# A diffusion backbone on one core: the first stage in one written order, with bands by row and scale and gates turned from columns

## The chip, the core and the metric

The kernel runs on one core of one Trainium2 chip. The time is device microseconds of one execution; the median of the runs is compared. The engines are named as the profile names them: PE (TensorE, matmuls), DVE (VectorE), ACT (ScalarE), POOL (GpSimd) and SP (SyncE, which issues the loads and stores here). SBUF is the memory that the engines work from, PSUM the banks that PE writes.

## The reference

512 latent tokens `x` and 256 context tokens `ctx`, each of 1024 features, go through two layers; everything is float32. Layer 0 mixes tokens by pooling, layer 1 by attention, and each is followed by an MLP of width 4096. Six vectors per layer (shift, scale and gate of the mixer and of the MLP) come from the conditioning, once for the latent and once for the context tokens. The first layer's mixer and what surrounds it:

```
sh1, sc1, gt1, sh2, sc2, gt2 = split(silu(c) @ w_ada[i] + b_ada[i], 6)      # c_ctx gives the context's
h   = rms_norm(x, g_mix_pre) * (1 + sc1) + sh1
# pooling: feature group g (256 features) averages over a window of 2, 4, 8 or 16 tokens
y   = concat_g((mean_g(h) - h)[:, group g] @ w_pool[g]) * pool_scale
x   = x + gt1 * rms_norm(y, g_mix_post)
m   = rms_norm(x, g_mlp_pre) * (1 + sc2) + sh2
x   = x + gt2 * rms_norm(square(relu(m @ w_in)) @ w_out, g_mlp_post)
```

`rms_norm(x, g)` is `x * rsqrt(mean(x*x) + eps) * g`. `pool_scale` and the gate `gt1` are vectors over the 1024 features, the same for all tokens of a kind.

## The kernel before, in words

Tokens stand in rows of 128: four latent rows (0 to 3) and two context rows (4 and 5), each a tile of 128 tokens by 1024 features in `xr`. Features are cut into eight tiles of 128 (k = 0 to 7), two for each window of the pooling. Matrix products whose weights are float32 are made of parts: weights and activations are split into a high part and a remainder (`hi`, `lo`), and three products of parts are added in PSUM.

The first stage is everything from the first load to the first group of the MLP's input matmuls. It runs thus:

- **Row norms.** Each row is loaded (`xload`, issued by SP), ACT squares and sums it, DVE adds epsilon, POOL raises to the power -0.5, and DVE writes the scaled row into `acc`. `rows_a` issues the first three, `rows_b` the last.
- **Bands.** The mean of a window minus the token itself is a product with a band matrix of 128 by 144. `band_mm(t, ks)` multiplies row t's feature tiles ks by it, into PSUM tiles named psm (latent) and psc (context), with features on the partitions; neighbouring rows add into the same columns, so a feature tile is complete when its last row is done. The bands of a first and of a last row have other edges: `band_edge(0)` and `band_edge(1)` each make a copy of the band and change its edge, both on DVE. `band_ev` moves the sums to SBUF.
- **Conditioning.** For each of the vectors PE multiplies weights from `w_ada` (1 MB per load, PSUM tile psada) by the conditioning; DVE adds rows, PE selects (`sel`), DVE and ACT finish.
- **Mixer.** The sums are scaled by 1 + sc1 and split (`hi` on ACT, `lo` on DVE), and multiplied by the split pooling weights (pspool). Before the split, the pooling weights are multiplied by `pool_scale`, which has to stand in every partition: `pool_weights` makes that by a matmul of a column of ones, on one partition, with the 4 KB row `scale_row` (psg).
- **Gates.** A gate is a column of 128 features per tile, and it is needed as a row in every partition. `gate_half(ci, h)` makes four tiles of it by a matmul of the column, read with a stride of 0 over 128 columns, with the identity (psg). The attention's gate (`gate_rows`, line 333) uses the same function.
- **Turns.** The rows are transposed for the MLP (psx), split, and its first group is multiplied (psin).

PE executes its instructions in one order, and the first stage's order is written out by hand. `Steps` holds pairs of a time and a function, and runs them sorted by that time; the string `FIRST` is a list of some 300 steps, each put in at 14.5 and a running thousandth. Ahead of these stand, by times of their own, the row norms, the bands of the first four feature tiles for the four latent rows, and the pool scale. While the stage is issued, PE, DVE and ACT are wrapped in `Kept`, which pins what they issue into program order (hence the many instructions whose line is that of this helper: 89 before, 91 after). Behind the stage a scheduler orders DVE and ACT.

Loads of weights go into two pools of buffers (`rawe` with four, `rawp` with three); which load of the first stage takes which is set by the list `turns`. PSUM is two double banks (psA) and four single ones (psB).

Of the kernel before, what the change touches and what calls it, by code (L numbers as in the profile page):

```python
# [9 lines left out]
F32 = mybir.dt.float32  # L10
# [3 lines left out]
ALU = mybir.AluOpType  # L14
# [27 lines left out]
ev:0* ev:2 psc0:4 psm:4 rb:5 wsc:0 psm:6 wsc:1 ev:4* wph:0 mm:SC1_0 wph:1 wpl:0 mm:SH1_0 ev:6* rows:SC1_0 wpl:1  # L42
psc0:5 sel:SC1_0 rows:SH1_0 evc:2* mods:SC1_0 evc:0* sel:SH1_0 mm:SC1_1 mods:SH1_0 hi:0 psc:4 rows:SC1_1 hi:1
psc:6 lo:0 mm:SH1_1 evc:4* lo:1 evc:6* sel:SC1_1 rows:SH1_1 pool:4:0 mods:SC1_1 sel:SH1_1 mm:SC1_2 mods:SH1_1
hi:2 pool:0:0 rows:SC1_2 pool:5:0 hi:3 lo:2 mm:SH1_2 lo:3 sel:SC1_2 rows:SH1_2 pool:4:1 mods:SC1_2 sel:SH1_2
ms:4:0 mm:SC1_3 mods:SH1_2 hi:4 c:4:0 pool:5:1 rows:SC1_3 mm:SH1_3 hi:5 lo:4 sel:SC1_3 pool:0:1 rows:SH1_3
mods:SC1_3 sel:SH1_3 lo:5 pool:1:0 pool:1:1 mods:SH1_3 pool:5:2 hi:6 mm:GT1_0a ms:1:0 lo:6 pool:4:2 hi:7
mm:GT1_0b c:1:0 lo:7 pool:0:2 mm:GT1_2a rows:GT1_0 pool:4:3 sel:GT1_0 ms:4:1 mm:GT1_2b w_in mods:GT1_0 gc:0:0
gc:1:0 c:4:1* rs:4 pool:0:3 rows:GT1_2 psg:0:0 ms:0 sel:GT1_2 psg:1:0 c:0* mods:GT1_2 rs:0 gc:0:1 gc:1:1 psg:1:1
gate:1:0 gate:0:0 pool:5:3 b:4:0 gate:1:1 b:1:0 mm:SC2_0a ms:5 b:4:1 psg:0:1 r:4 c:5* rs:5 pool:1:2 gate:0:1 b:5  # L50
mm:SC2_0b s:4 pool:1:3 r:5 whi:0 rs2:4 pool:3:0 ms:1:1 rows:SC2_0 pool:3:1 c:1:1* b:0 mm:SH2_0a rs:1 n:4*
sel:SC2_0 b:1:1 mm:SH2_0b s:5 r:0 pool:2:0 whi:1 rs2:5 pool:2:1 rows:SH2_0 pool:2:2 s:0 mods:SC2_0 r:1 sel:SH2_0
mm:SC2_2 n:5* rs2:0 mods:SH2_0 wlo:0 pool:2:3 s:1 turn:4:0 n:0 turn:4:1 ms:2 rs2:1 mm:SH2_2 h:4:1 h:4:0* rs:2
pool:3:2 n:1 xhi:4:0 mm:SC2_3 rows:SH2_2 xhi:4:1 rows:SC2_2 xlo:4:0 sel:SH2_2 turn:0:1 xlo:4:1 sel:SC2_2 h:0:1*
pool:3:3 mods:SH2_2 mods:SC2_2 turn:0:0 b:2 xhi:0:1 mm:SH2_3 ms:3 xlo:0:1 in:4:0:1 h:0:0* rows:SH2_3 rs:3
in:4:1:1 b:3 xhi:0:0 in:0:1:1 r:3 turn:0:2 in:4:0:0 h:0:2* xlo:0:0 in:4:1:0 s:3 r:2 in:0:1:0 in:0:0:1 xhi:0:2
rs2:3 wlo:1 s:2 in:0:0:0 turn:0:3 xlo:0:2 n:3* sel:SH2_3 rs2:2 turn:4:2 rows:SC2_3 in:0:2:0 mods:SH2_3 h:4:2*
n:2 sel:SC2_3 in:0:2:1 xhi:4:2 mods:SC2_3 turn:2:2 h:0:3 turn:4:3 h:2:2* turn:2:3 xlo:4:2 turn:2:1 xhi:2:2 h:4:3
in:4:2:1 h:2:1* in:4:2:0 xlo:2:2 xhi:4:3 h:2:3 turn:2:0 in:2:2:1 xhi:2:1 xlo:4:3 xhi:0:3 in:2:2:0 xlo:2:1 h:2:0*
in:4:3:1 xlo:0:3 in:2:1:0 xhi:2:0 xhi:2:3 in:0:3:1 xlo:2:0 xlo:2:3 in:0:3:0 in:4:3:0 in:2:0:0 in:2:3:0 in:2:0:1  # L60
in:2:3:1 in:2:1:1
# [31 lines left out]
def backbone(ctx: ExitStack, tc, x, ctx_in, w_ada, w_pool, pool_scale, w_qkv, g_q, g_k, w_o, w_mlp_in,  # L93
# [134 lines left out]
    given = phase[:, 16:32]  # L228
    sy.dma_start(given, vecs[:, 160:176])
# [10 lines left out]
    one = sm_tile("sm")  # L240
    ve.memset(one, 1.0)
# [87 lines left out]
    def gate_half(ci, h):  # L329
        ps = psB.tile([P, 512], F32, tag="b", name="psg")  # L330
        gc = halfgate.pop((ci, h))
        for k in range(4):
            te.matmul(ps[:, k * P:(k + 1) * P], gc[:, 4 * h + k:4 * h + k + 1].broadcast_to([P, P]), ident,
                      start=True, stop=True)
        halfgate[ci, h] = ps
# [105 lines left out]
    def band_edge(v):  # L441
        c = (HALO, P)[v]
        ve.tensor_copy(bands[:, v], bands[:, 2])
        ve.tensor_copy(bands[:, v, :, c:c + HALO], edges[:, v])

    band_edge(0)

    means, lat, con = {}, {}, {}

    def band_open(k):  # L450
        lat[k] = psA.tile([P, 2, 512], F32, tag="a", name="psm")
        for u in range(2):
            means[k + u] = lat[k][:, u, :], None

    def band_open_c(k):
        con[k] = psB.tile([P, 2, 256], F32, tag="b", name="psc")
        for u in range(2):
            means[k + u] = means[k + u][0], con[k][:, u, :]

    def band_mm(t, ks):  # L460
# [4 lines left out]
        for k in ks:  # L465
# [3 lines left out]
    def band_ev(k, q, on_act):  # L469
        to = accv[:, (0, NL)[q]:(NL, NT)[q], P * k:P * k + 256]  # L470
        (sc.copy if on_act else ve.tensor_copy)(to, (lat, con)[q][k].rearrange("p u (a n) -> p (u a) n", n=256))
        for u in range(2):
            means[k + u] = (means[k + u][0], to[:, u, :]) if q else (to[:, 2 * u:2 * u + 2, :], means[k + u][1])
# [1138 lines left out]
```

## Time and profile before

| what | us |
|---|---|
| median of 3 runs | 1158.05 (1158.02 to 1160.07) |
| the profiled execution | 1160.61 |
| its span | 1158.80 |
| PE busy (of the span) | 1142.9 (99%) |
| DVE busy | 932.9 (81%) |
| ACT busy | 632.8 (55%) |
| end of the first stage: the second group of the MLP's input matmuls starts on PE | 96.58 |

The page's first part gives each engine's busy time; a matmul of float32 parts leaves one record, and one of plain float32 leaves two. In a timeline a row is the start and the duration of a run of equal instructions on one engine, the operation and its output and input; in brackets stand the idle time ahead of it and what released it. The chain of waits runs from the last instruction back, at each step to what released it.

### The profile page before, as it was taken

The numbers are of one execution on the slowest core, as the hardware profiler recorded it, in microseconds if no ns is written. First come the engines' busy times: TensorE is split into PE (matmuls) and PEld (weight loads), VectorE is DVE, ScalarE is ACT, GpSimd is POOL, SyncE is SP. The second block draws the span as 40 slices with busy tenths as digits, with TensorE's granted clock in tenths as the row PEclk, the third lists the DMA queues.
The fourth block names the chain that finished last, engine by engine and source line by source line (L and its number), as shares of the span: only waits on it lengthen the run. The fifth ranks groups of instructions, "written<-read, shape, count | busy, mean of one in ns | idle before, by whom it ended". The sixth has DMA issues, their size and how long they took to land.

```text
span 1158.8 us, 16048 instructions
## 1 busy us (share of the span) xinstructions
PE 1142.9 (99%) x6220; PEld 992.7 (86%) x6220; DVE 932.9 (81%) x1522; ACT 632.8 (55%) x1076; POOL 69.7 (6%) x113
## 2 busy tenths in 40 slices
PE   7999999999999999999999999999999999999997
PEld 5789899898898988998888889998988888888886
DVE  4699588889988997996777699867687679778876
ACT  5687555555354534555675367753676436534523
POOL 1050000000000000000242200001100000000001
PEclk9999999999999999999999999999999999999999
DMA  9973222334344444343522102115244214313212
GB/s 374 419 282 140 73 103 107 130 139 143 112 146 146 145 146 145 109 146 109 182 74 73 37 1 74 37 74 186 105 141 150 77 69 146 109 40 142 109 32 114
DMA packets 25518, 147.34 MB, mean 127 GB/s; under 512 B 2785, under 2 KB 5345, under 8 KB 9698
## 3 DMA queue, kind: packets, MB, share of 16 engines
q1 hardware_dynamic: 25442, 146.32, 34.8%
q8 instruction: 49, 0.80, 0.3%
q14 instruction: 27, 0.22, 0.1%
HBM read 138.96 MB, written 7.34 MB: 126 GB/s over the span
## 4 chain that ended last, share of the span: by engine, by line
PE 91%; issue 2%; DVE 2%; ACT 2%; POOL 2%; DMA 1%; SPq 0%; POOLq 0%; DVEq 0%; ACTq 0%
PE pso L890 24%; PE psin L745 18%; PE psin L621 16%; PE pso L1001 12%; PE psy L1427 3%; PE po L1402 3%; PE pss L1361 3%; PE psq L1147 2%; PE pspt L1383 2%; PE pspool L89 2%; PE psada L89 2%; PE psin L89 2%; PE psm L89 1%; PE psx L89 1%; PE psg L89 1%
## 5 line engine op out<-in xcount | busy, mean ns | idle before, releaser
L890 PE MATMUL pso<-units,rb 128*128 128x512 f32 x1152 | 278.5, 392 | 0.0
L890 PEld LDWEIGHTS pso<-units,rb 128*128 128x128 f32 x1152 | 214.8, 188 | 41.2
L304 DVE SCALAR_TENSOR_TENSOR rows<-raw,cond,rows 128x256 f32<-128x256 f32 x280 | 127.5, 480 | 2.0
L904 DVE TENSOR_TENSOR acc<-acc,pso 128x512 f32<-128x512 f32 x126 | 84.0, 682 | 40.8 <-PE pso L890 40.7
L621 PE MATMUL psin<-ra,rb 128*128 128x512 f32 (+1 forms) x310 | 87.8, 360 | 0.0
L1001 PE MATMUL pso<-units,pairs 128*128 128x512 f32 x336 | 82.6, 389 | 0.0
L621 PE MATMUL psin<-ra 128*128 128x512 f32 (+1 forms) x256 | 76.5, 376 | 0.0
L1001 PEld LDWEIGHTS pso<-units,pairs 128*128 128x128 f32 x336 | 63.1, 188 | 13.1
L1005 DVE TENSOR_TENSOR acc<-acc,pso 128x512 f32<-128x512 f32 x72 | 48.7, 683 | 26.3 <-PE pso L1001 26.3
L212 POOL TENSOR_SCALAR ms<-ss 128x1 f32<-128x1 f32 x15 | 10.4, 691 | 969.6 <-ACT junk L199 924.1
L745 PE MATMUL psin<-ra,units 128*128 128x384 f32 x336 | 65.6, 337 | 0.4 <-ACT psin L757 0.4
L745 PE MATMUL psin<-sums,units 128*128 128x384 f32 x336 | 64.1, 337 | 0.0
L745 PEld LDWEIGHTS psin<-ra,units 128*128 128x128 f32 x336 | 59.7, 188 | 4.0 <-ACT psin L757 0.9
L621 PEld LDWEIGHTS psin<-ra,rb 128*128 128x128 f32 x310 | 55.6, 189 | 8.7
L745 PEld LDWEIGHTS psin<-sums,units 128*128 128x128 f32 x336 | 58.9, 188 | 1.6
L171 DVE TENSOR_TENSOR units<-raw,units 128x1024 fp32r<-128x1024 f32 (+2 forms) x49 | 55.2, 1152 | 4.9 <-ACT units L168 4.8
L621 PE MATMUL psin<-rb 128*128 128x512 f32 (+1 forms) x155 | 55.8, 361 | 0.6 <-DVE rb L1496 0.6
L168 ACT CAST units<-raw 128x1024 fp32r<-128x1024 f32 (+2 forms) x49 | 46.8, 995 | 16.9 <-PE pso L890 12.8
L621 PEld LDWEIGHTS psin<-ra 128*128 128x128 f32 x256 | 47.1, 188 | 8.8
L902 ACT COPY acc<-pso 128x512 f32<-128x512 f32 x48 | 27.2, 588 | 48.7 <-PE pso L890 48.4
L1147 PE MATMUL psq<-units,ra 128*128 128x512 f32 x216 | 52.2, 393 | 0.0
L621 PE MATMUL psin<-rb,ra 128*128 128x512 f32 (+1 forms) x128 | 48.1, 376 | 0.0
(292 smaller groups left out, 2395.0 us busy)
## 6 DMA issues: line engine op xcount, KB each, us to landing
raw<-in_w_ada SPq DMA_DIRECT2D x48, 1024.0 KB, 5.1
raw<-in_w_mlp_in SPq DMA_DIRECT2D x32, 1024.0 KB, 4.9
raw<-in_w_mlp_out SPq DMA_DIRECT2D x32, 1024.0 KB, 5.0
raw<-in_w_qkv SPq DMA_DIRECT2D x6, 1024.0 KB, 5.0
spill<-xr SPq DMA_DIRECT2D x10, 512.0 KB, 5.5
xr<-spill SPq DMA_DIRECT2D x10, 512.0 KB, 7.0
raw<-in_w_o SPq DMA_DIRECT2D x4, 1024.0 KB, 4.9
xr<-in_x SPq DMA_DIRECT2D x4, 512.0 KB, 6.5
```

Source lines behind the costliest of these rows:

```text
L89: return lambda *args, **kw: self.tc.keep_in_program_order(f(*args, **kw))
L168: a = sc.copy(hi, raw)
L171: b = ve.tensor_tensor(out=lo, in0=raw, in1=hi, op=ALU.subtract)
L304: ve.scalar_tensor_tensor(out=r, in0=raw[:, k, :], scalar=cond[:, k, c:c + 1], in1=r, op0=ALU.mult, op1=ALU.add)
L621: te.matmul(ps[:, bank, o:o + ln], w[:, k, fs], rhs, start=start, stop=(k == KT - 1 and n == 2), skip_group_check=len(ks) < KT or self.paired)
L745: te.matmul(bank, w[k], a[k], start=start and k == 0 and m == 0, stop=stop and k == 3 and m == 2, skip_group_check=True)
L890: te.matmul(pss[h][:, 0:cols[h][1]], a[:, f, ts_], w[:, f, cols[h][0]:sum(cols[h])], start=(n == 0 and not seeded[t]), stop=(n == len(seq) ...
L904: ve.tensor_tensor(out=d, in0=d, in1=ps[:, 0:w], op=ALU.add)
L1001: te.matmul(ps, a, w, start=(m == 0), stop=(m == len(seq) - 1))
L1005: ve.tensor_tensor(out=M[n][:, t], in0=M[n][:, t], in1=ps, op=ALU.add)
L1147: te.matmul(ps, a[:, k, sl], w[:, k % 4, :], start=(k == 0 and n == 0), stop=(k == KT - 1 and n == 2))
L1361: te.matmul(ps[:, c2, 0:384], a[:, sl], b[:, kv, 384 * c2:384 * c2 + 384], start=(n == 0), stop=(n == 2))
```

## The change

The first stage's whole order now comes from `FIRST`, from the first row on.

- The row norms become four kinds of steps (`xs` square, `xe` epsilon, `xp` power, `xn` scaled row) and stand in the list by themselves. Row 4's scaled row moves from DVE to ACT (a star marks ACT).
- The band edges become steps: `edge:0` stays on DVE and stands behind row 1's epsilon, `edge:1` moves to ACT.
- A step `psm:t:k` multiplies row t's feature tiles k and k + 1. All eight feature tiles of the latent rows are worked as the rows come, where four were before and the other four followed behind the rows. For them all eight PSUM banks are held: tiles 0 to 3 in the two double banks, 4 to 7 each in a single one, evacuated in pieces of 128 by 512. The context's bands (`psc`) stand behind the first conditioning matmuls.
- Row 1 is loaded ahead of the bands.
- The pool scale is no row any more. It rides as eight columns in the first small load (`phase[:, 32:40]`), and `pool_weights` turns them by eight transposes; the load of 4 KB, the two matmuls with ones, and the tile of ones go.
- `gate_half` uses four transposes in place of four matmuls with the identity, in the first stage and for the attention's gate.
- `turns` is another list, `pool_a` takes its two single banks one by one, and the steps of the conditioning, mixer, gates and turns stand in another order.

The diff, cut to its core; of the list the first lines stand for all.

```diff
 FIRST = """
-ev:0* ev:2 psc0:4 psm:4 rb:5 wsc:0 psm:6 wsc:1 ev:4* wph:0 mm:SC1_0 wph:1 wpl:0 mm:SH1_0 ev:6* rows:SC1_0 wpl:1
...
+xs:0 xe:0 xp:0 xn:0 xs:1 xe:1 xs:2 edge:0 xp:1 psm:0:2 xn:1 xs:3 psm:0:0 xe:2 psm:0:4 xp:2 psm:1:2 xs:4 xn:2
+psm:1:4 psm:0:6 xe:3 xp:3 edge:1* psm:2:4 xe:4 psm:2:2 xp:4 xn:3 xs:5 psm:1:0 psm:3:4 psm:3:2 ev:4* xe:5 psm:2:0
...
-    given = phase[:, 16:32]
-    sy.dma_start(given, vecs[:, 160:176])
+    given, pool_cols = phase[:, 16:32], phase[:, 32:40]
+    sy.dma_start(phase[:, 16:40], vecs[:, 160:184])
...
     xload(0)
-    scale_row = work_tile()[0:1]
-    sy.dma_start(scale_row, pool_scale[0:1])
+    xload(1)
     sy.dma_start(gate.rearrange("p a n -> p (a n)")[:, 8 * BW:12 * BW + 64], band)
-    for t in range(1, NT):
+    for t in range(2, NT):
         xload(t)
...
         for k in range(4):
-            te.matmul(ps[:, k * P:(k + 1) * P], gc[:, 4 * h + k:4 * h + k + 1].broadcast_to([P, P]), ident,
-                      start=True, stop=True)
+            te.transpose(ps[:, k * P:(k + 1) * P], gc[:, 4 * h + k:4 * h + k + 1].broadcast_to([P, P]), ident)
...
-    def band_edge(v):
-        c = (HALO, P)[v]
-        ve.tensor_copy(bands[:, v], bands[:, 2])
-        ve.tensor_copy(bands[:, v, :, c:c + HALO], edges[:, v])
-
-    band_edge(0)
+    def band_edge(v, on_act):
+        c, copy = (HALO, P)[v], sc.copy if on_act else ve.tensor_copy
+        copy(bands[:, v], bands[:, 2])
+        copy(bands[:, v, :, c:c + HALO], edges[:, v])
...
     def band_open(k):
-        lat[k] = psA.tile([P, 2, 512], F32, tag="a", name="psm")
+        if k < 4:
+            lat[k] = psA.tile([P, 2, 512], F32, tag="a", name="psm")
         for u in range(2):
-            means[k + u] = lat[k][:, u, :], None
+            if k >= 4:
+                lat[k + u] = psB.tile([P, 512], F32, tag="b", name="psm")
+            means[k + u][0] = lat[k][:, u, :] if k < 4 else lat[k + u]
...
-    def rows_a(t):
-        ss, ms, rs[t] = sm_tile("ss"), sm_tile("ms"), sm_tile("rs")
-        mean_square(xr[:, t, :], ss[:, 0:1])
-        ve.tensor_scalar(out=ms[:, 0:1], in0=ss[:, 0:1], scalar1=EPS, scalar2=None, op0=ALU.add)
-        gp.tensor_tensor(out=rs[t][:, 0:1], in0=ms[:, 0:1], in1=nhalf[:, 0:1], op=ALU.pow)
-
-    def rows_b(t):
-        scaled(accv[:, t, :], t, rs[t])
...
+    def row_scaled(t, on_act):
+        if on_act:
+            sc.activation(accv[:, t, :], xr[:, t, :], AF.Copy, scale=rs[t][:, 0:1])
+        else:
+            scaled(accv[:, t, :], t, rs[t])
...
     def pool_weights(h):
         ps = psB.tile([P, 512], F32, tag="b", name="psg")
-        te.matmul(ps, one[0:1, 0:1].broadcast_to([1, P]), scale_row[:, 512 * h:512 * h + 512], start=True, stop=True)
-        pw.append(ps)
+        for k in range(4):
+            te.transpose(ps[:, k * P:(k + 1) * P], pool_cols[:, 4 * h + k:4 * h + k + 1].broadcast_to([P, P]), ident)
+        pooled_scale[h] = ps
...
-    turns.extend((0, 0, 0, 0, 1, 1, 0, 0, 1, 0, 0, 1, 0, 0, 1, 0, 0, 1, 0, 0))
+    turns.extend((0, 0, 0, 0, 1, 1, 0, 0, 0, 0, 1, 1, 0, 0, 0, 0, 1, 1, 0, 0))
...
-    st.at(0.1, pool_weights, 0)
...
-    st.at(7.9, pool_weights, 1)
-    st.at(6.85, band_edge, 1)
-    st.at(14, pool_load)
+    st.at(0.5, pool_load)
...
     for n, what in enumerate(FIRST.split()):
-        st.at(14.5 + n / 1000, step, what)
+        st.at(1 + n / 1000, step, what)
```

What stands on PE at its start, before the change. psg on `work` is the pool scale's matmul with ones, psm the latent bands, psc the context's; the numbers behind a name are partitions and columns of the output.

```order
L89 MATMUL psg<-work,sm 128x512
L89 MATMUL psm<-gate,acc 128x136 x4
L89 MATMUL psm<-gate,acc 128x144 x4
L89 MATMUL psg<-work,sm 128x512
L89 MATMUL psm<-gate,acc 128x144 x4
L89 MATMUL psm<-gate,acc 128x136 x4
L89 MATMUL psc<-gate,acc 128x136 x4
L89 MATMUL psm<-gate,acc 128x136 x2
L89 MATMUL psm<-gate,acc 128x144 x4
L89 MATMUL psm<-gate,acc 128x136 x4
L89 MATMUL psm<-gate,acc 128x144 x4
L89 MATMUL psm<-gate,acc 128x136 x2
```
And after it, where psg on `phase` are the transposes of the scale's columns and psada is the first conditioning:

```order
L91 MATMUL psm<-gate,acc 128x136 x6
L91 MATMUL psm<-gate,acc 128x144 x4
L91 MATMUL psm<-gate,acc 128x136 x2
L91 MATMUL psm<-gate,acc 128x144 x6
L91 MATMUL psm<-gate,acc 128x136 x4
L91 MATMUL psm<-gate,acc 128x144 x2
L91 MATMUL psm<-gate,acc 128x136 x2
L91 MATMUL psg<-ident,phase 128x128 x4
L91 MATMUL psm<-gate,acc 128x144 x4
L91 MATMUL psm<-gate,acc 128x136 x2
L91 MATMUL psg<-ident,phase 128x128 x4
L91 MATMUL psada<-raw,cond 32x256 x8
```
The 32 latent band matmuls, 16 by rows and 16 behind them, were ahead of the conditioning and are so now, all by rows: six of the first row lead, where four did; the four of the context among them and the scale's two on one row are gone from there, and the scale's eight transposes came.

What stands on DVE from its first work on the rows, before; the two COPY are a band edge, ms is the mean square plus epsilon, and acc on `xr` is the scaled row:

```order
L443 COPY gate<-gate 128x576
L444 COPY gate<-gate 128x4x8
L89 TENSOR_SCALAR ms<-ss 128x1
L89 TENSOR_SCALAR acc<-xr,rs 128x1024
L89 TENSOR_SCALAR ms<-ss 128x1
L89 TENSOR_SCALAR acc<-xr,rs 128x1024
L89 COPY gate<-gate 128x576
L89 COPY gate<-gate 128x4x8
```
And after:

```order
L91 TENSOR_SCALAR ms<-ss 128x1
L91 TENSOR_SCALAR acc<-xr,rs 128x1024
L91 TENSOR_SCALAR ms<-ss 128x1
L91 COPY gate<-gate 128x576
L91 COPY gate<-gate 128x4x8
L91 TENSOR_SCALAR acc<-xr,rs 128x1024
L91 TENSOR_SCALAR ms<-ss 128x1
L91 TENSOR_SCALAR acc<-xr,rs 128x1024
L91 TENSOR_SCALAR ms<-ss 128x1 x2
```
The first edge moved from ahead of row 0's epsilon to behind row 1's epsilon, and the second edge left DVE.

What SP issues first, before and after:

```order
L229 DMA phase<-in_vecs 128x16
L232 DMA xr<-in_x 128x1024
L235 DMA work<-in_pool_scale 1x1024
L236 DMA gate<-in_band 128x640
L232 DMA xr<-in_x 128x1024 x3
L232 DMA xr<-in_ctx 128x1024 x2
L239 DMA vec<-in_vecs 128x160
```
```order
L231 DMA phase<-in_vecs 128x24
L234 DMA xr<-in_x 128x1024 x2
L237 DMA gate<-in_band 128x640
L234 DMA xr<-in_x 128x1024 x2
L234 DMA xr<-in_ctx 128x1024 x2
L240 DMA vec<-in_vecs 128x160
L151 DMA raw<-in_w_pool 128x2048
```
The scale's load is gone, and row 1 and the band have changed places.

More of the change, by code (lines that the diff above doesn't have):

```diff
@@ L47 @@
[L47 to L56, printed above, removed]
@@ L834, in backbone @@
     kinds = dict(
-        rb=rows_b, psc0=lambda t: band_mm(t, range(4)), psm=band_rows, psc=band_context,
+        xs=row_square, xe=row_eps, xp=row_pow, xn=row_scaled, edge=band_edge, psm=band_mm, psc=band_mm, pw=pool_weights,
         ev=lambda k, act: band_ev(k, 0, act), evc=lambda k, act: band_ev(k, 1, act),
```

104 lines of the change are left out of this document (56 added, 48 removed).

## The prediction

> **What bounds the kernel now.** I read the page first, for the engine that carries the span, then the chain, then the groups of PE in the stretch that the change rewrites, then PE's waits behind it.
>
> ```profile
> PE 1142.9 (99%) x6220; PEld 992.7 (86%) x6220; DVE 932.9 (81%) x1522; ACT 632.8 (55%) x1076; POOL 69.7 (6%) x113
> PE 91%; issue 2%; DVE 2%; ACT 2%; POOL 2%; DMA 1%; SPq 0%; POOLq 0%; DVEq 0%; ACTq 0%
> ...
> PE pss L1361 <- ACT gate L1366: 0.6, 2, 0.4
> PE psin L621 <- DVE rb L1496: 0.6, 1, 0.6
> PE psin L745 <- ACT psin L757: 0.4, 1, 0.4
> PE psq L1147 <- DVE ra L411: 0.3, 1, 0.3
> ```
>
> The last four rows are all of PE's waits from 96 us to the end: 1.9 us in 1062. Behind the first stage nothing but PE sets the time, so what PE gains in the first stage reaches the end, unless a new wait appears. The first stage in PE's groups (0 to 97 us; the last column is PE's idle time before the group):
>
> ```profile
> L89 PE MATMUL psm<-gate,acc 128*128 128x144 f32 x32 | 6.9, 377 | 1.1 <-DVE acc L89 1.1
> L89 PE MATMUL psx<-ident,acc 128*128 128x128 f32 x48 | 6.7, 275 | 0.0
> L89 PE MATMUL psm<-gate,acc 128*128 128x136 f32 x32 | 6.3, 352 | 0.9 <-DVE acc L89 0.9
> L89 PE MATMUL psg<-ident,gc 128*128 128x128 f32 x32 | 4.5, 283 | 0.3 <-DVE gc L89 0.3
> L89 PE MATMUL psg<-work,sm 1*128 1x512 f32 x4 | 4.1, 1129 | 5.1 <-DMA work<-in_pool_scale 5.1
> ```
>
> A float32 matmul leaves two records and a transpose one: 32 latent band matmuls stand here as 64 records (psm). Once the rows come, PE idles 1.1 us before the second row and 0.3 at the gates. So the stage is a sum of PE work, and the change is worth what it takes from that sum. Its course, from the timeline (start, us, what; the idle time before it in brackets):
>
> ```profile
> 5.02 1.06 ACT L89 ACTIVATE junk<-xr 128x1024 bf16<-128x1024 f32 x1 [0.91 <-DMA xr<-in_x]
> 5.12 2.04 PE L89 MATMUL psg<-work,sm 1*128 1x512 f32 x2 [5.12 <-DMA work<-in_pool_scale]
> 5.84 0.46 DVE L443 COPY gate<-gate 128x576 f32<-128x576 f32 x1 [4.07 <-DMA gate<-in_band]
> 6.33 0.18 DVE L444 COPY gate<-gate 128x32 f32<-128x32 f32 x1
> 8.06 2.18 PE L89 MATMUL psm<-gate,acc 128*128 128x136 f32 x8 [0.90 <-DVE acc L89]
> 8.55 1.06 ACT L89 ACTIVATE junk<-xr 128x1024 bf16<-128x1024 f32 x1 [2.38 <-DMA xr<-in_x]
> 9.73 0.15 DVE L89 TENSOR_SCALAR ms<-ss 128x1 f32<-128x1 f32 x1 [1.73 <-ACT junk L89]
> 11.36 2.29 PE L89 MATMUL psm<-gate,acc 128*128 128x144 f32 x8 [1.12 <-DVE acc L89]
> 13.58 2.07 PE L89 MATMUL psg<-work,sm 1*128 1x512 f32 x2
> 14.09 0.75 DVE L89 TENSOR_SCALAR acc<-xr,rs 128x1024 f32<-128x1024 f32 x1 [0.66 <-POOL rs L481]
> 15.58 3.87 PE L89 MATMUL psm<-gate,acc 128*128 128x144 f32 x16
> 19.29 1.09 PE L89 MATMUL psc<-gate,acc 128*128 128x136 f32 x8
> 20.22 3.98 PE L89 MATMUL psm<-gate,acc 128*128 128x136 f32 x32
> 24.12 1.93 PE L89 MATMUL psada<-raw,cond 128*32 128x256 f32 x32
> ...
> 49.52 1.04 PE L89 MATMUL psada<-raw,cond 128*32 128x512 f32 x8
> ...
> 74.05 1.07 PE L89 MATMUL psada<-raw,cond 128*32 128x256 f32 x16
> ...
> 96.58 16.81 PE L621 MATMUL psin<-ra,units 128*128 128x384 f32 x96
> ```
>
> Read the pace from the starts: from 15.58 to 19.29 sixteen records, 0.23 us each; from 20.22 to 24.12 thirty-two, 0.12 each. The same band matmul costs 0.46 us before about 19.2 us and 0.24 after it. The stage ends at 96.58, where PE begins the second group of the MLP.
>
> **The change on PE.** The pieces of the chain give the price of a form on the path (start, us, what):
>
> ```profile
> 13.65 2.00 PE psg L89 x2
> ...
> 51.47 0.89 PE psg L89 x8
> ...
> 73.68 0.44 PE psx L89 x4
> ...
> 769.33 0.22 PE psg L333 x2
> ...
> 770.62 1.56 PE psg L333 x14
> ```
>
> Eight records of four gate matmuls cost 0.89 us; four transposes, the form that the change puts in their place, 0.44 (the psx row: the same 128x128 float32 against the identity). The Trainium skill ("TensorE: Matmul & The Clock Gate", Terms) calls the transpose mode four times faster for float32; by that, four would take 0.22 and the sum below 1.8 us less, but the psx row says half, and I use the row.
>
> Gates of the first stage: four groups, 4 x (0.89 - 0.44) = -1.8 us, all on the path. `gate_half` also serves the attention gate (L333): 16 records, 1.78 us on the path, become 8 transposes, 0.88: -0.9 us.
>
> Pool scale: two matmuls on one row of ones, 2 us each, go. The one at 5.12 lay before the first row had come and returns nothing; the one at 13.58 lay between rows, -2.0. Eight transposes come, +0.9, and they stand on the path. Its load of 4 KB goes too (0.33 us of SP's issue, beside transfers); the columns ride in the first load.
>
> Bands (psm are the latent bands, psc the context's; PE's first rows stand in the section on the change): the 32 latent ones stand ahead of the conditioning as before, but all by rows, six of the first row's first where four were. By eight for each row PE has 16 to do while row 2 arrives, so I take it that it no longer waits for a row. What may come later is its start, which hangs on DVE. The edge now stands behind row 1's epsilon, so PE's first matmul waits for the arrival of row 1, plus 1.2 us of square (from its start at 8.55 to DVE's epsilon at 9.73), 0.15 of epsilon and 0.65 of copies. Row 1 is now loaded ahead of the bands. Bounds: as late as now (8.5), or one load of 512 KB at 0.4 MB per us behind row 0 (6.3); PE then starts between 8.3 and 10.5, and I take 9.5, the middle.
>
> From there: before, 24.12 - 8.06 = 16.1 us hold the 32 band matmuls, four of the context, 2.0 of scale and 1.1 of idle. After, I need the moment at which the pace changes. In this trace it came 7.8 us after the last idle gap (11.36), and 3.6 us after the one-row matmul ended (15.58). PE works without gap from 9.5 now, so the change lies between 13.1 and the old 19.2; I take 16. Then 6.5 us at 0.46 do 14 matmuls, 18 at 0.24 take 4.3, the transposes 0.9 and a switch of form 0.2: the conditioning starts at 21.4, not 24.1. Four context matmuls that were ahead now follow, +0.9 (psc at 19.29 to 20.22). Bands and scale together: -1.8 us.
>
> Waits: the chain of each feature pair (row transpose on DVE, selection, scale on ACT, remainder on DVE, pool on PE) is as long as before, in another order. I put +0.2 on it, by the 0.3 that PE idles at the gates now; ends: 0 and 1.5. ACT takes one edge and row 4's scaling from DVE, behind row squares that wait for transfers anyway; four evacuations of 128x512 replace two of 128x1024 beside PE's bands. If that cover is gone, the cost is in the 1.5.
>
> Of the first loads on SP, beside the scale's, only row 1 and the bands change places. Whether the weights keep up is read from the windows (the last two columns are the DMA's busy share and GB/s):
>
> ```profile
> 65.00:70.00 5.00, 5.00 (x66) 3.53 (x64) 4.31 (x9) 4.78 (x9) 4.46 (x7) 1.00 1.01 416
> 70.00:75.00 5.00, 5.00 (x72) 3.62 (x68) 4.88 (x11) 3.79 (x7) 1.16 (x2) 1.00 0.42 167
> ```
>
> The queue is full until about 72 us, at 1 MB per 2.5 us. The last in it is a weight of the MLP; the last conditioning weight landed about 69.6, and the twelfth (the gates' last), nine loads earlier, about 47.1, an estimate. PE took that one at 49.52: 2.4 us of room. With 2.2 of gate work removed behind it, the stage cannot gain more than some 5 us whatever PE does.
>
> **Sum.** -1.8 (bands, scale) - 1.8 (gates) + 0.2 (waits) - 0.9 (attention) = -4.3 us. The profiled execution took 1160.61 us (span 1158.80 and 1.81 around it), 2.6 above the median of the runs, 1158.05; against it the sum gives 1156.3, and on the median 1153.7.
>
> **Rivals.** (1) The pace changes late, at 19.2 as now or later: 9.7 us at 0.46 are 21 matmuls, the conditioning starts at 23.1, and the total is -2.7, 1155.4. For it: one trace knows only one moment. Against it: that moment followed on work with gaps.
> (2) The pace changes early. In the trace 3.6 us of unbroken full matmuls preceded the change; counted from 9.5 that is 13.1, the conditioning starts at 20.1, and the total is -5.6, close to the limit of the loads: 1152.4. The Trainium skill (the same page, Part 1) says that the array's clock is halved by default and released after one busy window of about 3.4 us, free-running, so within 3.4 to 6.8 us of steady work. By that rule the change comes at 12.9 to 16.3. That the row's granted clock is 1.00 throughout agrees with a gate that this column doesn't show.
> (3) A transpose of a column read with stride 0 is no cheaper than the matmul: the gates return nothing, the scale costs 1.8. Total -0.7: 1157.4. The psx row was measured on full tiles, so it can't exclude it.
> (4) The gain is kept, then lost: DVE is busy 81% of the span, and the order of DVE and ACT also shifts in the first groups of the MLP. A wait of 2 to 4 us there gives 1156 to 1158. Against it: PE has no such wait now.
> (5) Slower: the order in which the two buffer pools are taken (`turns`) changes, so a load may wait for a buffer that PE frees late. One hole in the full queue moves every later landing by what it lasts. The last conditioning weight landed at 69.6 and PE took it at 74.05, which is 4.4 us of room: a hole of 4.4 us makes the change worth nothing, one of 6.7 us makes it tell as slower, and one of 10 gives 1164. Against it: the queue has no hole now, and 16 of the list's 20 loads keep their pool.
>
> **Chances.** Forecast (the pace between 14 and 18 us, 1152.8 to 1154.8) 0.45; (1) 0.18; (2) 0.14; (3) 0.06; (4) 0.11; (5) 0.06. A measurement of this kernel tells about 0.2%, 2.3 us. Faster: the forecast, (2) and most of (1) and a little of (4), 0.76; same: the rest of (1), (3) and (4), 0.18; slower 0.06. The range leaves out (5), half of (3) and the ends of (2): 1151.8 to 1157.0.
>
> **What would show it.** The second group of the MLP at about 93.2 us, not 96.6; the conditioning at about 21.4; psg groups of four records at 0.44; the pace change before 19; PE's waits behind 96 us still about 2 us. A start of the bands past 10.5, an idle gap of PE over 1 us between 22 and 96, a psg group at 0.89, or waits of over 2 us behind 96 would make it wrong.

## The result and the profile after

| | before | after |
|---|---|---|
| median (range, runs), us | 1159.06 (1158.02 to 1162.18, 6) | 1155.20 (1155.15 to 1155.88, 6) |
| profiled execution, us | 1160.61 | 1155.58 |
| its span, us | 1158.8 | 1153.7 |
| first stage ends, us | 96.58 | 92.39 |

The ratio is 0.9955, with a 95% interval of 0.9945 to 0.9965. A second set, beside the experiments, gave 0.9965 (0.9953 to 0.9978), with the changed kernel at 1155.78 (1155.47 to 1156.05). One run of the kernel before in that second set took 4045.56 us and is left out of its ratio. Of the 5.1 us between the two spans, 4.2 lie in the first stage and 0.9 in the attention's gate.

First, the changed kernel's busy times (PEld is PE's loading of weights), and all its PE waits of 0.3 us and more (us in total, how many, longest):

```profile
PE 1135.3 (98%) x6200; PEld 988.7 (86%) x6200; DVE 930.9 (81%) x1517; ACT 632.1 (55%) x1082; POOL 71.1 (6%) x113
```

```profile
PE psm L91 <- DVE gate L91: 8.3, 1, 8.3
PE psx L91 <- DVE acc L91: 1.2, 2, 0.6
PE pss L1355 <- ACT gate L1360: 0.6, 2, 0.4
PE psin L637 <- DVE rb L1490: 0.6, 1, 0.6
PE psin L761 <- ACT psin L773: 0.4, 1, 0.4
PE psq L1141 <- DVE ra L409: 0.4, 1, 0.4
PE psx L91 <- ACT acc L91: 0.3, 1, 0.3
PE psada L91 <- DVE mods L91: 0.3, 1, 0.3
```

Behind the first stage nothing changed: the waits of pss, psin and psq are the ones of before. Inside it, PE starts at 8.3 us and no longer waits for a row, but behind the start of the conditioning it waits 1.7 us (psx and psada) where it waited 0.3 before, for the gates. Then the course of the stage, in rows picked from the timeline:

```profile
6.18 1.06 ACT L91 ACTIVATE junk<-xr 128x1024 bf16<-128x1024 f32 x1 [0.21 <-DMA xr<-in_x]
8.29 9.27 PE L91 MATMUL psm<-gate,acc 128*128 128x136 f32 x52 [8.29 <-DVE gate L91]
17.40 0.60 PE L91 MATMUL psg<-ident,phase 128*128 128x128 f32 x4
...
19.81 1.07 PE L91 MATMUL psada<-raw,cond 128*32 128x256 f32 x16
33.52 1.07 PE L91 MATMUL psada<-raw,cond 128*32 128x256 f32 x16
45.49 0.65 PE L91 MATMUL psg<-ident,gc 128*128 128x128 f32 x4
45.89 0.96 PE L91 MATMUL pspool<-rb,ra 128*128 128x256 f32 x6
62.38 0.55 PE L91 MATMUL psx<-ident,acc 128*128 128x128 f32 x3 [0.65 <-DVE acc L91]
67.97 0.98 PE L91 MATMUL psx<-ident,acc 128*128 128x128 f32 x7 [0.52 <-DVE acc L91]
92.39 7.79 PE L637 MATMUL psin<-ra,units 128*128 128x384 f32 x44
```

ACT starts on row 1 at 6.18 (8.55 before; below, this start is called its arrival), the bands run without a gap from 8.29, the conditioning starts at 19.81 (24.12), and the second group of the MLP at 92.39 (96.58). A gate's four transposes take 0.36 to 0.40 us to the next instruction. The attention's gate, in the chain:

```profile
765.05 0.11 PE psg L332
...
765.39 0.11 PE psg L332
...
766.33 0.66 PE psg L332 x6
```

Eight records, 0.88 us, where sixteen took 1.78.

**Where the first stage's 4.2 us came from.** From the start of the conditioning to the stage's end it is 96.58 - 24.12 = 72.5 us before and 92.39 - 19.81 = 72.6 after. So by position the whole gain stands ahead of the conditioning. Behind it, from each PE instruction's start to the next, added up by tile: gates -2.4, pooling matmuls -0.7 (in 14 unbroken runs, not 17), against the context's bands +1.5 (four that stood ahead, and five runs, not two), new waits +1.4 (1.7 less 0.3), turns and the MLP's first group +0.5, the conditioning's own matmuls -0.1.

**What bounds it now.** The seventh conditioning weight is used at 33.52, and before the change it was used at 37.37:

```profile
37.37 1.05 PE L89 MATMUL psada<-raw,cond 128*32 128x256 f32 x16
```

Its load on SP, before and after (SPq is the instruction that issues it, the window holds this issue, and the last number is us to landing):

```profile
raw<-in_w_ada SPq DMA_DIRECT2D x1, 1024.0 KB, 8.5
```

```profile
raw<-in_w_ada SPq DMA_DIRECT2D x1, 1024.0 KB, 12.4
```

Issued at 25.25, it landed at 33.71 before, and PE took it at 37.37: 3.7 us of room. After, it was issued at 20.94 and landed at 33.38, and PE took it 0.14 later, which is also the distance in the executions below where PE does wait for a weight. PE has caught up with the loads. The eighth weight stands as close: it landed at 35.98 and was taken at 36.13. Before, that load's landing is missing from the trace; by its neighbours (33.71 and 39.66, 2.5 us a load) it lies at 36.2 to 37.2, and PE took it at 39.25, an estimate of 2.1 to 3.1 us of room.

### The profile page after: what moved, and what is told of

The parts are those of the page before. It is cut to its first block, busy times and chain, and to the rows that moved or that the text cites. A ratio compares the mean times of both kernels' runs of the same rounds, so it can differ in the third digit from the quotient of the medians.

```text
span 1153.7 us, 16000 instructions
## 1 busy us (share of the span) xinstructions
PE 1135.3 (98%) x6200; PEld 988.7 (86%) x6200; DVE 930.9 (81%) x1517; ACT 632.1 (55%) x1082; POOL 71.1 (6%) x113
## 4 chain that ended last, share of the span: by engine, by line
PE 90%; issue 3%; POOL 3%; DVE 2%; ACT 2%; DMA 0%; POOLq 0%; DVEq 0%; SPq 0%; ACTq 0%
PE pso L884 24%; PE psin L761 18%; PE psin L637 16%; PE pso L995 12%; PE psy L1421 3%; PE po L1396 3%; PE pss L1355 3%; PE psq L1141 2%; PE pspt L1377 2%; PE psin L91 2%; PE psada L91 1%; POOL rs L216 1%; PE psm L91 1%; PE pspool L91 1%; POOL rs L1150 1%
## 5 line engine op out<-in xcount | busy, mean ns | idle before, releaser
L170 ACT CAST units<-raw 128x1024 fp32r<-128x1024 f32 (+2 forms) x49 | 47.0, 995 | 17.6 <-PE pso L884 13.4
```

The costliest lines, as they stand in the source:

```text
L170: a = sc.copy(hi, raw)
```

## The experiments

In the table "clock" is the moment from which a record of PE takes half as long (a record of a band matmul 0.12 us, not 0.23); the trace's records of the granted clock begin at the same moment. "Seventh" is the use of the seventh weight, its landing in brackets. The first five columns are from one profiled execution each; the median, its range and the ratio are of all runs. Each ratio is to the kernel before in its own set of runs, whose median lay between 1159.06 and 1161.22 from set to set, so ratios compare better than medians of different sets. The two kernels at the head are those of the result above.

| kernel | clock | conditioning | seventh (landed) | stage ends | median us (range) | ratio (95%) |
|---|---|---|---|---|---|---|
| before | 19.1 | 24.12 | 37.37 (33.71) | 96.58 | 1159.06 (1158.02 to 1162.18) | |
| after | 14.1 | 19.81 | 33.52 (33.38) | 92.39 | 1155.20 (1155.15 to 1155.88) | 0.9955 (0.9945 to 0.9965) |
| gates_mm | 13.9 | 19.65 | 33.71 (33.58) | 93.20 | 1157.33 (1157.18 to 1157.40) | 0.997 (0.996 to 0.998) |
| row_load | 11.9 | 18.77 | 33.85 (33.72) | 93.01 | 1155.62 (1155.19 to 1156.06) | 0.9959 (0.9944 to 0.9974) |
| warm_after | 6.4 | 17.84 | 33.93 (33.80) | 92.82 | 1155.86 (1155.40 to 1156.11) | 0.996 (0.9946 to 0.9974) |
| reorder2 | 13.4 | 19.50 | 33.78 (33.65) | 91.80 | 1154.91 (1154.75 to 1155.97) | 0.9955 (0.994 to 0.997) |
| band_first | 14.3 | 20.38 | 34.07 (33.57) | 92.95 | 1156.56 (1156.02 to 1156.90) | 0.9974 (0.9962 to 0.9985) |
| before_gates_tr | 19.8 | 24.51 | 37.75 (33.90) | 95.16 | 1158.27 (1156.16 to 1159.21) | 0.9981 (0.9972 to 0.999) |
| before_cols | 14.1 | 20.40 | 34.19 (34.05) | 94.01 | 1157.63 (1157.48 to 1158.18) | 0.9982 (0.9973 to 0.9991) |
| both_small | 13.3 | 19.95 | 33.52 (33.38) | 92.25 | 1155.85 (1155.46 to 1156.21) | 0.9966 (0.9953 to 0.9979) |
| order_only | 13.4 | 20.92 | 34.61 (33.75) | 94.06 | 1158.05 (1157.52 to 1158.53) | 0.9984 (0.9975 to 0.9992) |
| one_row | 13.2 | 21.16 | 34.40 (33.48) | 93.62 | 1157.82 (1157.63 to 1161.19) | 0.9982 (0.9972 to 0.9991) |
| warm_before | 4.3, 21.4 | 25.24 | 38.47 (34.98) | 97.68 | 1158.46 (1157.46 to 1161.70) | 0.9989 (0.9978 to 1.0) |

### From the changed kernel: what each thing is worth there

**gates_mm**, the gates as before:

```diff
-            te.transpose(ps[:, k * P:(k + 1) * P], gc[:, 4 * h + k:4 * h + k + 1].broadcast_to([P, P]), ident)
+            te.matmul(ps[:, k * P:(k + 1) * P], gc[:, 4 * h + k:4 * h + k + 1].broadcast_to([P, P]), ident,
+                      start=True, stop=True)
```

> The changed kernel with the gates made by matmuls with the identity again (first stage and attention). If PE's sum sets the stage: each of the four groups costs about 0.98 us in place of 0.38, so the stage ends 2.4 us later (94.8 in place of 92.4), the attention's gate 0.9 more, 3.3 us in all against the changed kernel. Rival: PE's 1.7 us of waits between 61 and 68 us hang on the chains of row norms and take up the later PE work: the stage 0.7 later, 1.6 us in all.

Measured: the span is 1.9 us longer (1155.6 against 1153.7), 0.8 in the stage and 0.9 in the attention, and the median 2.1 (1.6 against the second set's 1155.78). The wait for the rows' norms became shorter:

```profile
PE psx L91 <- DVE acc L91: 0.5, 1, 0.5
...
PE psx L91 <- ACT acc L91: 0.3, 1, 0.3
```

The rival held: of the waits' 1.7 us, 0.8 are left, so half of what the slower gates cost had been standing there as a wait. In this order the gates are worth 0.8 in the stage, not 2.4; against after_again below, whose seventh weight landed as late as here (33.60 and 33.58), it is 0.5.

**row_load**, one 4 KB row loaded behind row 0, read by nothing:

```diff
     xload(0)
+    sy.dma_start(work_tile()[0:1], x[0, 0:1, :])
     xload(1)
```

> The changed kernel with a load of one 4 KB row into one partition put back behind the first row's load; nothing reads it. If that load is what held back every later landing by 1.27 us in the kernel before: row 1 lands near 7.4 in place of 6.10, the first conditioning weight at 18.8 in place of 17.5, PE starts 1.2 later and waits 1.1 us for the seventh weight (0.14 us of room now), and the time is 1.1 us longer. Rival: 4 KB at 400 GB/s is 0.01 us; landings and time stay as they are.

Measured: neither. Row 1 arrives at 6.26 in place of 6.18, but the first weight lands 0.35 us later (17.87 against 17.52). In the changed kernel's other variants without such a row it lands at 17.47 to 17.71, and in order_only, which has one, at 17.88, so the delay is 0.2 to 0.4. At the seventh weight it is not told apart: 33.72 here, 33.38 to 33.80 without. PE, which by the earlier clock reached the conditioning at 18.77, waits for weights:

```profile
26.54 1.07 PE L91 MATMUL psada<-raw,cond 128*32 128x256 f32 x16 [0.86 <-DMA raw<-in_w_ada]
```

The stage ends 0.6 later (0.3 against after_again), and the median lies between the changed kernel's two, 1155.20 and 1155.78. A load of 4 KB in one partition costs the full queue 0.2 to 0.4 us here, 20 to 40 times its bytes at 400 GB/s.

**warm_after**, dummy transposes ahead of the first band:

```diff
+    def warm(n):
+        ps = psB.tile([P, 512], F32, tag="b", name="pswarm")
+        for k in range(n):
+            te.transpose(ps[:, k % 4 * P:(k % 4 + 1) * P], ident, ident)
...
+    st.at(0.05, warm, 34)
```

> The changed kernel with 34 transposes of the identity on PE, from 1.5 us on, ahead of the first band; nothing reads them. If steady PE work of any kind sets the pace: the band matmuls run at 0.12 us a record from before 9 us on, and conditioning starts at 17.6 to 18 in place of 19.8. If the loads then bind (0.14 us of room at the seventh weight), the time falls by 0.1 to 0.3 us only and new PE waits of about 2 us on weights stand before 34 us. If PE's sum alone binds, it falls by 2.2 us. If transposes do not count, the pace changes near 14 us as now and nothing moves.

Measured: the clock as the first theory had it, and the time nearly as the second: nothing is gained (1155.86 beside 1155.20 and 1155.78).

```profile
8.37 4.91 PE L91 MATMUL psm<-gate,acc 128*128 128x136 f32 x36 [0.65 <-DVE gate L91]
17.84 1.07 PE L91 MATMUL psada<-raw,cond 128*32 128x256 f32 x16
20.33 1.07 PE L91 MATMUL psada<-raw,cond 128*32 128x256 f32 x16 [0.76 <-DMA raw<-in_w_ada]
26.19 1.07 PE L91 MATMUL psada<-raw,cond 128*32 128x256 f32 x16 [0.67 <-DMA raw<-in_w_ada]
33.93 1.07 PE L91 MATMUL psada<-raw,cond 128*32 128x256 f32 x16 [0.40 <-DMA raw<-in_w_ada]
92.82 7.45 PE L642 MATMUL psin<-ra,units 128*128 128x384 f32 x42
```

Conditioning starts 2.0 us earlier, and all of it is given back in three waits for weights, 1.8 us. The seventh landed 0.4 later in this execution, and the stage ends 0.4 later. From the seventh landing to the end it is 59.0 us in both. That the loads bind the changed kernel is shown by this run.

**band_first**, the band ahead of row 1 again:

```diff
     xload(0)
-    xload(1)
     sy.dma_start(gate.rearrange("p a n -> p (a n)")[:, 8 * BW:12 * BW + 64], band)
+    xload(1)
```

> The changed kernel with the band loaded ahead of row 1, as before. By bytes row 1 lands at 6.9 in place of 6.10, PE starts at 9.1 in place of 8.3, and since conditioning then starts 0.4 to 0.8 later, with 0.14 us of room at the seventh weight, the stage ends 0.3 to 0.7 later. If this order was what held back the loads of the kernel before by 1.27 us, row 1 lands near 8.4, the seventh weight near 34.3, PE starts at 10.4, and the stage ends 1.0 to 1.5 later. Rival: the loads bind so far that nothing moves.

Measured: row 1 arrives at 7.24, PE starts at 9.22, conditioning at 20.38, and the stage ends 0.56 later: the first case. The order of these loads is worth about 0.5 us of the stage (0.3 against after_again), and it is not what held row 1 back to 8.55 before.

**reorder2**, five steps of the list moved (the list's lines are shown from the first moved step on):

```diff
-sel:SC2_0 n:4* turn:0:1 rows:SH2_0 mm:SC2_2 s:5 mods:SC2_0 sel:SH2_0 rows:SC2_2 pool:3:3 mods:SH2_0 rs2:5 b:2
-h:0:1* turn:0:0 sel:SC2_2 mm:SH2_2 h:0:0* n:5 mods:SC2_2 turn:4:0
+sel:SC2_0 rows:SH2_0 pool:3:3 mm:SC2_2 turn:0:1 s:5 mods:SC2_0 mm:SH2_2 sel:SH2_0 rows:SC2_2 mods:SH2_0 rs2:5 n:4* b:2
+h:0:1* turn:0:0 sel:SC2_2 h:0:0* n:5 mods:SC2_2 mm:SC2_3 turn:4:0
...
-sel:SH2_2 mm:SC2_3 mods:SH2_2
+sel:SH2_2 mods:SH2_2
```

> The changed kernel with a few steps of the list moved between 61 and 69 us: the last pooling group and two conditioning matmuls go ahead of the turns of rows that PE waits for, a third ahead of the next turn, and row 5's square goes ahead of row 4's scaled row on ACT. If PE's 1.7 us of waits there were a matter of order: they shrink to below 0.6 and the stage ends 1.0 to 1.7 us earlier. Rival: the chains of row norms set the time whatever PE does meanwhile: the wait moves to the first matmuls of the MLP and the time stays within 0.3 us.

Measured: between the two. The waits in this stretch fell from 1.7 to 0.8 us:

```profile
PE psx L91 <- DVE mods L91: 0.3, 1, 0.3
PE psin L91 <- DVE acc L91: 0.2, 1, 0.2
PE psada L91 <- ACT acc L91: 0.2, 1, 0.2
```

The stage ends 0.6 earlier; 0.9 counted from the seventh landing, which was 0.3 later in this execution. So half of the waits were order. In the median it is 0.3 us (1154.91 against 1155.20, and 1155.78 in the second set), with ranges that overlap: the lowest median of all kernels, but not told apart from the changed one.

### From the kernel before: which part carries the gain

**before_gates_tr**, only the gates by transposes (the edit of gates_mm, the other way).

> The kernel before with nothing but the gates made by transposes. By their price in the changed kernel (0.38 us a group in place of 0.98, four in the first stage and four in the attention) and no PE wait to swallow it, the stage ends 1.9 to 2.4 us earlier (94.2 to 94.7 in place of 96.58) and the time falls by 2.8 to 3.3 us. Rival: as in the changed kernel, chains of row norms between 60 and 70 us give new waits, and only 0.8 + 0.9 = 1.7 us come out.

Measured: between the two cases. The span is 2.3 us shorter, 1.4 in the stage and 0.9 in the attention. In this execution the clock changed 0.7 later than in that of before, and conditioning began 0.4 later; from there to the end it is 1.8 us less. No new wait stood behind it. The gates' own price, 2.0 us from start to start, comes out here nearly in full. The likely reason is that PE has room at its weights (3.9 us at the seventh) and waits only 0.4 us behind them.

**before_cols**, only the pool scale:

```diff
-    scale_row = work_tile()[0:1]
-    sy.dma_start(scale_row, pool_scale[0:1])
...
-        te.matmul(ps, one[0:1, 0:1].broadcast_to([1, P]), scale_row[:, 512 * h:512 * h + 512], start=True, stop=True)
+        for k in range(4):
+            te.transpose(ps[:, k * P:(k + 1) * P], pool_cols[:, 4 * h + k:4 * h + k + 1].broadcast_to([P, P]), ident)
```

> The kernel before with nothing but the pool scale turned from columns and its 4 KB load gone. PE's sum alone: 2.0 us of one-row matmul go and 0.9 of transposes come, -1.1. If the one-row matmul also held the pace back (steady work then counts from 11.4 us and the pace changes between 15 and 18 in place of 19.3), 0.5 to 1.4 more, the stage ending between 94.1 and 95.0. If the 4 KB row ahead of the bands was what made row 1 land at 8.46, row 1 lands near 7.2, PE no longer idles 1.1 us before row 1's bands, and the first conditioning weight lands near 17.5; if it was the order of row 1 and the bands, row 1 stays at 8.1 to 8.4.

Measured: the stage ends 2.6 us earlier, more than any sum of the instructions gives.

```profile
7.50 1.06 ACT L89 ACTIVATE junk<-xr 128x1024 bf16<-128x1024 f32 x1 [1.50 <-DMA xr<-in_x]
```

```profile
10.31 2.29 PE L89 MATMUL psm<-gate,acc 128*128 128x144 f32 x8 [0.25 <-DVE acc L89]
12.39 1.06 PE L89 MATMUL psg<-ident,phase 128*128 128x128 f32 x4
13.24 2.48 PE L89 MATMUL psm<-gate,acc 128*128 128x144 f32 x16
20.40 1.93 PE L89 MATMUL psada<-raw,cond 128*32 128x256 f32 x32
94.01 6.23 PE L618 MATMUL psin<-ra,units 128*128 128x384 f32 x35
```

Three things come together: row 1 arrives 1.05 us earlier (7.50, not 8.55) and PE idles 0.25 for it, not 1.1; the one-row matmul's 2.0 become 0.85; and the clock changes at 14.1, not 19.1. Conditioning starts 3.7 earlier. How much each of the three brings, this run doesn't separate. Then PE meets the loads: the seventh weight is taken 0.14 behind its landing, and 0.5 us of waits for weights, at the eighth, are new.

**both_small**, the two edits together and nothing else.

> The kernel before with the two small edits together: the pool scale turned from columns (its 4 KB load gone) and the gates made by transposes; the order of the first stage, the bands and the loads otherwise as before. Alone they ended the stage at 94.0 and 95.2 in place of 96.6. If the two carry the whole change and add up, the stage ends at 92.2 to 92.8, as in the changed kernel (92.4), and the times of the two agree within 0.7 us. Rival: the new order by rows carries 1 us or more of its own, and the stage ends at 93.4 or later.

Measured: the first case. The median is 1155.85 (1155.46 to 1156.21) beside 1155.78 of the changed kernel in the same set, the spans 1153.7 beside 1153.7 and 1154.0.

```profile
PE psada L89 <- DMA raw<-in_w_ada: 1.0, 2, 0.5
```

```profile
19.95 1.93 PE L89 MATMUL psada<-raw,cond 128*32 128x256 f32 x32
33.52 1.07 PE L89 MATMUL psada<-raw,cond 128*32 128x256 f32 x16 [0.17 <-PE psada L89]
92.25 5.02 PE L617 MATMUL psin<-ra,units 128*128 128x384 f32 x28
```

It reaches the seventh weight at the same 33.52 and ends at 92.25. Here too PE waits for weights (1.0 us); it has none of the waits for norms. The order by rows with its bands, its edges and its list adds nothing that can be measured to the two small edits.

**order_only**, the converse: the changed kernel with the scale's row and both kinds of matmul back.

> The changed kernel with both small edits undone: the pool scale by two matmuls on one row of ones again (at the places of its transposes, with the 4 KB load behind the first row) and the gates by matmuls with the identity; what is left of the change is the order by rows, the bands, the edges and the order of the loads. If the order is worth nothing by itself, it lies within 0.8 us of the kernel before in the median. If the order is worth what the two edits did not explain by their instructions (the earlier pace, no waits for rows), the one-row matmuls cost 1 to 2 us and the gates 0.8 and 0.9, and it lies 1 to 2.5 us below the kernel before.

Measured: 1158.05 beside 1160.36 for the kernel before in the same set, 1.9 us by the ratio, the second case. The earlier start by rows brings the clock to 13.4 and the conditioning to 20.92. The one-row matmuls are cheap there:

```profile
17.18 1.12 PE L91 MATMUL psg<-work,sm 1*128 1x512 f32 x2
18.23 1.71 PE L91 MATMUL psm<-gate,acc 128*128 128x144 f32 x12
```

At the fast clock one takes 1.05 us to the next instruction, not 2.0. So the order has a worth of its own (2.5 us of the stage). It is much the same worth that the columns have, PE at the seventh weight by 34.2 to 34.6 us, and most of it can be had only once: gates_mm, which is order and columns together, ends the stage 0.8 earlier than the columns alone (93.20 against 94.01).

**one_row**, before_cols with one matmul on ones put back behind the second transposes.

```diff
+    def one_row():
+        ps = psB.tile([P, 512], F32, tag="b", name="psone")
+        te.matmul(ps, one[0:1, 0:1].broadcast_to([1, P]), xr[0:1, 0, 0:512], start=True, stop=True)
...
+    st.at(7.95, one_row)
```

> The kernel before with the pool scale from columns, as above, and one matmul on a row of ones put back behind the second four transposes; its row is taken from the first latent row, so no load comes with it, and nothing reads its output. If a one-row matmul does not count as work for the pace, the pace changes 3 to 6 us behind its end at about 15.3, so between 18.3 and 21, in place of 14.2, conditioning starts at 23.5 to 24.5 in place of 20.4, and the stage ends 1.5 to 2.5 us later than 94.0 or at the landing of the weights, whichever is later. If it counts as any other, the pace changes between 14 and 17.2, and conditioning starts at 21.5 to 22.8.

Measured: it doesn't decide what it was made for.

```profile
13.27 1.12 PE L89 MATMUL psone<-xr,sm 1*128 1x512 f32 x2
14.32 2.17 PE L89 MATMUL psm<-gate,acc 128*128 128x144 f32 x16
```

Row 1 came early enough in this execution for PE not to idle at all from 8.27, the clock changed at 13.2, ahead of the one-row matmul, and it took 1.05 us. It does say something else: conditioning starts 0.8 us later than without it (20.40), and the stage ends no later (93.62 against 94.01; the seventh weight landed 0.6 earlier). Counted from that landing it ends 0.2 later, which is also the difference of the medians (1157.82 and 1157.63). One more microsecond of PE ahead of the loads costs some 0.2 us.

**warm_before**, the dummy transposes on the kernel before.

> The kernel before with 34 transposes of the identity on PE from 1.3 us on. The pace then changes before 8 us in place of 19.3, the first rows are waited for, and conditioning starts at about 21.8 in place of 24.1; the room at the weights is 2.4 us at the least, so the stage ends 1.8 to 2.4 us earlier and the time falls as much. If the moment of the pace is also what spreads the times of the kernel before (1158.0 to 1162.2), the times lie within 1 us of one another. Rival: the one-row matmul at 13.6 us turns the pace back, it changes near 19 us again, and nothing is won.

Measured: a median of 1158.46, 0.1% below before, and a spread of 4.2 us, not of 1. The profiled execution, the slowest of the ten, shows where its time went (windows of PE; the third column from the end is the granted clock):

```profile
8.00:9.00 1.00, 0.99 (x8) 1.00 0.98 381
9.00:10.00 1.00, 0.21 (x2) 1.00 1.02 414
10.00:11.00 1.00, 0.00 (x0) 1.00 1.02 418
11.00:12.00 1.00, 0.67 (x3) 0.58 1.05 423
...
20.00:21.00 1.00, 1.00 (x6) 0.50 1.00 418
21.00:22.00 1.00, 1.00 (x9) 0.80 1.02 426
```

The fast clock came at 4.3; then PE waited 2.1 us for row 1, the clock fell to 0.50 at 11.2 and rose again only at 21.4 (from 0.58 and 0.80 as means of their windows). A warm clock was lost in a wait of 2.1 us here, and was not lost in warm_after, whose waits ahead of the bands are 0.65 and 0.20. The other nine have only their mean granted clock on record. In four of the ten it is 0.995 or 0.996, and their times are 1159.59 to 1161.70 us; in the other six it is 0.998 or 0.999, as in the other kernels, and their times are 1157.46 to 1158.56. By this number four lost the clock, and the six that show no loss do as the first expectation has it: 2.5 us below the median of before in this set (1160.36), within 1.1 us of one another. That these six had the fast clock early and kept it fits, but is not shown: a late first rise doesn't show in this mean, and 7 of before's own 28 executions in this set lie as low (1157.68 to 1158.19). The rival's cause did not act in the profiled execution: the clock had fallen at 11.2, ahead of the one-row matmul at 13.5.

**after_again**, the changed kernel beside these.

> The changed kernel itself, to stand beside the others on the same chip: 1155.2 within 0.7 us, and the stage's end at 92.4 within 0.4, by how far the moment of the pace and the landings differ from one execution to the next.

Measured: 1155.78 in the median, and the stage ends at 92.69, with the seventh weight's landing 0.2 later than in the first execution.

## Why the prediction was right

The time fell as forecast: 1155.2 lies in the range, though above the forecast's own 1152.8 to 1154.8 and next to rival (1)'s 1155.4. The drop of the profiled execution, 5.0 us, stands beside the 4.3 of the sum. On the median it is 3.9, since the median of before rose from 1158.05 to 1159.06 with three more runs; in the second set, with before at 1160.36, it is 4.6. That the sum came out so close is luck in part: gains that were put too small and waits that were put far too small cancelled, and a bound that the sum doesn't hold, the loads, closed the rest.

- **Bands and scale, -1.8:** conditioning came 4.3 earlier, 3.4 with the four context matmuls counted at the prediction's 0.9 (the context's bands cost 1.5 more behind it than before). The step that was mis-sized is the start and the clock. PE started at 8.29, not 9.5, because row 1 arrived at 6.18: the early end of my bounds, not their middle. The clock changed at 14.1, not 16. The sentence that PE no longer waits for a row was right.
- **Row 1's arrival** I hung on its place in the queue alone. before_cols shows that 1.05 us of it belonged to the 4 KB load in the order of before, which I had costed at 0.33 of SP's issue, beside transfers; in the changed order such a load moved row 1 by 0.08 (row_load).
- **Gates, -1.8:** the price was right in kind (four transposes 0.38 us, four matmuls 0.98, taken from starts) and somewhat low: the same edit took 2.0 us of PE in the kernel before and 1.9 in the changed one. What came out of it in the changed order was 0.5 to 0.8.
- **Waits, +0.2, ends 0 and 1.5:** waits rose from 0.3 to 1.7 us, by 1.4, close to the upper end. This is the term that was furthest off for its size. I had taken the chain of each feature pair as unchanged; the waits were at the turns of rows, on the chains of row norms, and I had named nothing that would be late there once the gates ahead of them were faster. gates_mm shows the exchange: 1.9 us of gates for 0.8 of stage, with 0.9 of waits gone.
- **Attention, -0.9:** 1.78 became 0.88.
- **The limit of the loads, some 5 us:** right that there is one, and it is what set the result; wrong in its place. (The 2.2 us of gate work that I added behind it are 1.8 in my own sum.) I read the room at the twelfth weight, 2.4 us. It binds at the seventh and eighth, where before had 3.7 and some 2.1 to 3.1 us of room, because nearly all the gain lies ahead of them and the gates' gain behind. It should have been read at each weight against the gain up to there.

The rivals: (1), a late clock, is refuted by 14.1 (its own terms start the conditioning at 22.9, not 23.1). (2), an early clock near the loads' limit, happened in part: the clock lay between the forecast and this case, and so did the profiled execution's drop. (3) is refuted by gates_mm and before_gates_tr: a column read with stride 0 is turned at the speed of a full tile (0.36 to 0.40 us for four; the psx row has 0.44). (4) came true inside the first stage, not behind it. (5): no hole of that kind; the last conditioning weight was taken at 72.8, 4.5 us behind its landing.

What I had not asked at all is which part carries the gain. I summed the parts as independent. Columns and gates do add up: alone they bring 2.6 and 1.4 us of the stage, together 4.3. The order doesn't: by itself it brings 2.5 of the stage (1.9 us of the whole, by the ratio), on top of the columns 0.8, and on top of both nothing that can be measured.

## What to carry to other kernels

Where a queue of loads runs full beside an engine that is the bound, write down the room at every load against the gain expected up to it; the smallest difference caps the change, and parts that gain ahead of the same load add only in part. Take such a change apart before keeping its complicated half: here two edits of a few lines gave all of it. And a small load or a short wait at the start can cost more than its own time, when it decides when the clock rises.

## What the runs showed of the hardware

- **The clock's start does not show in the granted clock.** In the kernel before, the column stands at 1.00 while a band matmul takes 0.46 us, until 19 us:

```profile
17.00:18.00 1.00, 1.00 (x6) 1.00 1.06 442
```

  In warm_before the very same pace, six records in a microsecond, stands beside 0.50. So the slow start is the same throttle, from before the first change that the records know. I had guessed this in the prediction from the pace alone.
- **When it rises.** In the kernels whose PE works without a gap over 0.7 us from its first band or dummy on, it rose 3.0 to 6.2 us later (warm_before 1.3 to 4.3, row_load 8.3 to 11.9, after 8.3 to 14.1, before_cols 7.9 to 14.1). Where a one-row matmul stands in the slow stretch behind a wait of over 1 us, it took longer: before 11.4 to 19.1, before_gates_tr 11.4 to 19.8, warm_before 11.3 to 21.4. From the end of the one-row matmul at 15.5 to 15.6 these are 3.5, 4.2 and 5.9. That its time does not count as work fits all of these, but one_row missed the case, and before_cols took away the wait and the one-row matmul at once, so it stays open. The Trainium skill ("TensorE: Matmul & The Clock Gate", Part 1) gives one busy window of about 3.4 us, free-running, from which 3.4 to 6.8 us from a start is an estimate; the runs agree but for the 3.0. The Trainium skill (the same page, Part 4) says that the full clock doesn't come on for transposes; in warm_after and warm_before nothing but float32 transposes ran ahead, and it rose, at 6.4 and 4.3.
- **A 4 KB load into one partition** delayed the first weight behind it by 0.2 to 0.4 us in the changed order (row_load). In the order of before it was 0.8 to 1.2: that weight lands at 18.71 to 18.80 in the three kernels with the load (before, before_gates_tr, warm_before) and at 17.62 to 17.89 in the three without (before_cols, both_small, one_row). Why it is more there than in row_load was not settled.
- **Spread.** But for the one run named above, the kernel before lay between 1157.7 and 1162.2 over all sets, the changed one between 1155.15 and 1156.05. That the moment of the clock is free by some microseconds, and that the loads hide it after the change and not before, would do this; it was not shown.
